# Five pairs of split weights in place of four, the split three granules ahead in place of two, and eight weight buffers in place of nine

## The chip, the cores and the metric

The kernel runs on one core of one Trainium2 chip. The metric is the device time of one execution in microseconds. The engines are TensorE (PE; its weight loads are shown as PEld), VectorE (DVE), ScalarE (ACT), GpSimd (POOL) and SyncE (SP), which issues most DMA transfers.

## The reference

A trunk of two decoder layers on 256 positions of width 1024, in float32. Each layer adds to h, one after the other, a half-step SwiGLU FFN, a token mixer (differential attention in layer 0, a Mamba-2 SSD mixer in layer 1), a cross-attention into 256 memory tokens, and another half-step FFN; each works on an RMSNorm of h, and a final RMSNorm ends it.

```python
def swiglu(h, w_gate, w_up, w_down):
    return (jax.nn.silu(h @ w_gate) * (h @ w_up)) @ w_down
...
    for i in range(DEPTH):
        h = h + 0.5 * swiglu(rmsnorm(h, ffn1_norm[i]), ffn1_w_gate[i], ffn1_w_up[i], ffn1_w_down[i])
        hn = rmsnorm(h, mix_norm[i])
        ...
        h = h + memory_cross_attention(rmsnorm(h, xa_norm[i]), mem, xa_mem_norm[i],
                                       xa_w_q[i], xa_w_kv[i], xa_w_o[i])
        h = h + 0.5 * swiglu(rmsnorm(h, ffn2_norm[i]), ffn2_w_gate[i], ffn2_w_up[i], ffn2_w_down[i])
    return rmsnorm(h, final_norm)
```

An FFN has 2816 hidden units. All weights are read from HBM once, as float32.

## The kernel before

**The split.** Nearly every product with a weight is made of three matmuls on a shorter float format (`mm3`, lines 261 to 264): the weight and the other operand are each split into a high and a low part, and high by high, high by low and low by high are summed in PSUM. A weight arrives as a tile `w` of 128 partitions by 2048 (1 MB) in one of the buffers of pool `wp`. It is used in two *granules* of 1024 columns (class `Gran`; a few are smaller). `Gran.split` takes one pair of buffers from pool `hp`, loads the weight if that is not done yet, casts it on ACT to the high part `whi` (line 224), and subtracts on DVE to get the low part `wlo` (line 225; two granules of the very first product do it on POOL):

```python
            hi = hp.tile([P, 1024], F32R, name="whi", tag="hi")
            lo = hp.tile([P, 1024], F32R, name="wlo", tag="lo")
            ...
                nc.scalar.copy(hv, src)
                self.eng.tensor_tensor(self.lo[:, :, o:o + n], src, hv.bitcast(F32), op=ALU.subtract)
```

A pair is free again when the granule's last matmul is done, and a weight buffer when its last granule's low part is done.

**The lookahead.** The products are listed as `units`; all their granules stand in one list in the order of use, and each knows its place `at`. A product takes its granules through `use`, which first writes down the splits of all granules up to AHEAD further ones:

```python
    def ready(n):
        while done[0] < min(len(grans), n):
            grans[done[0]].split()
            done[0] += 1

    def use(gr):
        for g in gr:
            ready(g.at + AHEAD + 1)
            yield g
```

`last`, the final FFN's tail, calls `ready(gr[-1].at + AHEAD)` itself. Work that follows a product (moving results out of PSUM, transposes, softmax and so on) is put down through `pipe`, a clock of estimated PE time: a piece is written when the PE work written so far has reached its due time.

**Order.** In the first two units (the gate and the up product of the first 512 hidden columns) PE, DVE, ACT and SP run their instructions in the order in which they are written (`manual_schedule`). Afterwards the compiler's scheduler chooses each engine's order from priorities and its own estimates; in the SSD part PE's order is the written one again. At run time every engine works through its own queue.

**The start.** `begin` issues the first loads (the first weight in four pieces of 256 KB with the second half of x between them, then the second weight in two of 512 KB), writes the first four of eight rows of the normalized input (`xh`, `xl`, from `put`) and the splits of granules 0 to 2. The gate unit's eight granules have one row (512 columns) each. The other rows 4 to 7 come from `second`, due at 2.7 us of the pipe's clock, each with the splits up to its row (`ready(k + 1)` for rows 4 and 5); the squares for the norm's scale are due at 2.6 and 7.0.

**The FFN's blocks.** Most of the gate and up products are done in blocks of seven half-size products instead of eight (`seven`, lines 361 to 393). A block loads four weight tiles, of which some products need sums: `x1` is the sum of two tiles (`Sum.load`, line 203, on DVE, into a buffer of its own), `x2` adds a third to it (line 203 again, in place), `x3` and `x4` add by DMA from POOL's queue (line 199). A granule of a block is six matmuls of 512 columns; between them `share` puts granules of plain products with twelve matmuls, which need as much splitting for twice the matmul work. There are three such blocks in the first FFN, four in each of the other three, and one in each cross-attention.

Of the kernel before, what the change touches and what calls it, by code (L numbers as in the profile page):

```python
# [20 lines left out]
NHT = HID // P  # L21
EPS = 1e-6

AHEAD = 2

T = dict(gate=5.5, hid=3.0, turn=1.3, row=5.0, rot=5.5, probs=(1.0, 4.0, 7.0, 10.0), tp=8.5, heads=4.5, otp=6.5,
         xprobs=5.0, xtp=5.5, xo=3.0, evac=1.5)
# [30 lines left out]
def trunk(ctx, tc, a, out):  # L58
# [1 line left out]


    const = ctx.enter_context(tc.tile_pool(name="const", bufs=1))
    wp = ctx.enter_context(tc.tile_pool(name="wp", bufs=9))
    hp = ctx.enter_context(tc.tile_pool(name="hp", bufs=4))
    xp = ctx.enter_context(tc.tile_pool(name="xp", bufs=8))
    sp = ctx.enter_context(tc.tile_pool(name="sp", bufs=28))
    wk = ctx.enter_context(tc.tile_pool(name="wk", bufs=7))
# [163 lines left out]
# [11 lines that stand above are left out]
# [1294 lines left out]
    def last(norm):  # L1536
# [56 lines left out]
        def run(*gr):  # L1593
            ready(gr[-1].at + AHEAD)
            last_ = gr[-1].k0 + gr[-1].nk == 20
            for t, c0, c1 in [(0, 0, 512), (1, 0, 256), (1, 256, 512)]:
                if (t, c0) not in banks:
                    banks[t, c0] = acc("fin")[:, :c1 - c0]
                b = banks[t, c0]
                for g in gr:  # L1600
                    for k in range(g.nk):
                        kt = g.k0 + k
                        mms(b, t, g, k, slice(c0, c1), kt, kt == 12, kt == 19)
                if last_:
                    for q in range((c1 - c0) // 256):
                        evac(b[:, q * 256:(q + 1) * 256], t, 2 + c0 // 256 + q)
# [80 lines left out]
```

## Time and profile before

| | |
|---|---|
| median of 3 runs | 1257.57 us (1257.47 to 1257.57) |
| the profiled execution | 1258.38 us, span of its instructions 1256.6 us |
| busy: PE, PEld, DVE, ACT, POOL | 1247.1, 1071.7, 1057.2, 873.5, 162.5 us |
| granted clock | 0.999 |
| casts to high parts (line 224, ACT) | 534, 551.0 us |
| subtractions to low parts (line 225, DVE) | 532, 639.4 us |
| sums of weights (line 203, DVE) | 32, 73.2 us |
| read from HBM | 271.72 MB, 218 GB/s over the span |

Rows of the timeline give the start in us from the span's start, the length in us, the engine (a q behind its name: its queue issuing a DMA), the line, the operation, what it writes and reads, the shape, and in brackets how long the engine had been idle and what ended that. Rows of waits give who waited for whom, the sum in us, how often, and the longest. Rows of windows give the stretch, its length, each engine's busy time and number of instructions (PE, PEld, DVE, ACT, POOL), the granted clock, the mean busy share of the 16 DMA engines, and GB/s. Rows of groups give count, busy us, mean ns of one, and the engine's idle time just before them with what ended most of it.

### The profile page before, as it was taken

Reading aid. Unit: us, or ns where it says so; the run is one execution under the profiler, and the core shown is the slowest. Engines: PE = TensorE matmul, PEld = TensorE weight load, DVE = VectorE, ACT = ScalarE, POOL = GpSimd, SP = SyncE. Lnnn points to the kernel's source line nnn. Section 1 sums busy time; section 2 is a strip of 40 time slices with the busy share of each in tenths; the row PEclk is TensorE's granted clock in tenths of the full one; section 3 lists DMA queues with packets and bytes.
Section 4 is the critical chain, followed back from the end, with each engine's and each line's share of the span. In section 5 each row is a group of like instructions: output and inputs, shape, how many; then the busy total and the mean of one; then the engine's idle time right before and its main releaser. Section 6 shows DMA issues by size and latency. Waiting matters only on the chain.

```text
span 1256.6 us, 18186 instructions
## 1 busy us (share of the span) xinstructions
PE 1247.1 (99%) x6751; PEld 1071.7 (85%) x6751; DVE 1057.2 (84%) x1451; ACT 873.5 (70%) x1388; POOL 162.5 (13%) x139
## 2 busy tenths in 40 slices
PE   9999999999999999999999999999999999999997
PEld 7888888788998888888888889999998898888886
DVE  6998787887787999887998976798898887898886
ACT  6676764686676776767776756777876775877772
POOL 1101102101101111110111000022233100011100
PEclk9999999999999999999999999999999999999999
DMA  9989976445776688987879977665636586489961
GB/s 330 301 255 259 314 256 208 137 165 170 222 214 170 165 252 260 293 246 234 240 198 268 311 247 221 192 193 168 201 134 185 169 246 182 157 251 256 258 190 34
DMA packets 161195, 275.03 MB, mean 219 GB/s; under 512 B 7209, under 2 KB 43730, under 8 KB 161106
## 3 DMA queue, kind: packets, MB, share of 16 engines
q1 hardware_dynamic: 137744, 229.75, 53.4%
q0 software_dynamic: 19744, 38.28, 17.7%
q10 hardware_dynamic: 3618, 5.84, 1.4%
q8 instruction: 53, 0.87, 0.3%
q14 instruction: 36, 0.29, 0.1%
HBM read 271.72 MB, written 2.13 MB: 218 GB/s over the span
## 4 chain that ended last, share of the span: by engine, by line
PE 94%; DMA 2%; DVE 2%; ACT 2%; issue 1%; POOLq 0%; POOL 0%; SPq 0%; ACTq 0%; DVEq 0%
PE out L262 9%; PE out L264 9%; PE out L263 9%; PE seven L263 8%; PE seven L262 8%; PE seven L264 8%; PE htp L855 1%; PE up L263 1%; PE up L264 1%; PE up L262 1%; PE xs L264 1%; PE xs L262 1%; PE xq L263 1%; PE xq L264 1%; PE xs L263 1%; PE xq L262 1%
## 5 line engine op out<-in xcount | busy, mean ns | idle before, releaser
L225 DVE TENSOR_TENSOR wlo<-w,whi 128x1024 fp32r<-128x1024 f32 (+2 forms) x532 | 639.4, 1220 | 134.6 <-ACT whi L224 126.8
L224 ACT CAST whi<-w 128x1024 fp32r<-128x1024 f32 (+2 forms) x534 | 551.0, 1039 | 245.2 <-PE out L264 84.0
L262 PE MATMUL out<-whi,hid_hi 128*128 128x512 f32 x336 | 132.3, 394 | 0.0
L264 PE MATMUL out<-whi,hid_lo 128*128 128x512 f32 x336 | 131.0, 390 | 0.0
L263 PE MATMUL out<-wlo,hid_hi 128*128 128x512 f32 x336 | 130.8, 389 | 0.0
L263 PE MATMUL seven<-wlo,s_hi 128*128 128x512 f32 x272 | 106.0, 390 | 0.6 <-DVE wlo L225 0.6
L262 PE MATMUL seven<-whi,s_hi 128*128 128x512 f32 x272 | 106.2, 390 | 0.0
L264 PE MATMUL seven<-whi,s_lo 128*128 128x512 f32 x272 | 105.9, 389 | 0.0
L199 POOL DMA_DIRECT2D w<-in_ffn_w_up_dram x30 | 36.7, 1268 | 346.6 <-DVE wlo L225 339.5
L203 DVE TENSOR_TENSOR w<-w 128x2048 f32<-128x2048 f32 x32 | 73.2, 2287 | 2.0 <-DMA w<-in_ffn_w_gate_dram 1.5
L264 PEld LDWEIGHTS out<-whi,hid_lo 128*128 128x128 f32 x336 | 63.1, 188 | 13.4
L263 PEld LDWEIGHTS out<-wlo,hid_hi 128*128 128x128 f32 x336 | 63.1, 188 | 12.6
L262 PEld LDWEIGHTS out<-whi,hid_hi 128*128 128x128 f32 x336 | 63.1, 188 | 12.5
L262 PE MATMUL seven<-whi,xh 128*128 128x512 f32 x180 | 70.5, 392 | 0.0
L264 PE MATMUL seven<-whi,xl 128*128 128x512 f32 x180 | 70.1, 389 | 0.0
L263 PE MATMUL seven<-wlo,xh 128*128 128x512 f32 x180 | 70.0, 389 | 0.0
L263 PEld LDWEIGHTS seven<-wlo,s_hi 128*128 128x128 f32 x272 | 51.1, 188 | 11.4 <-DVE wlo L225 1.0
L264 PEld LDWEIGHTS seven<-whi,s_lo 128*128 128x128 f32 x272 | 51.1, 188 | 10.7
L262 PEld LDWEIGHTS seven<-whi,s_hi 128*128 128x128 f32 x272 | 51.1, 188 | 10.4
L199 POOL DMA_DIRECT2D w<-in_ffn_w_gate_dram x30 | 36.9, 1467 | 176.2 <-DVE xst L1146 62.3
L264 PEld LDWEIGHTS seven<-whi,xl 128*128 128x128 f32 x180 | 33.8, 188 | 7.1
L262 PEld LDWEIGHTS seven<-whi,xh 128*128 128x128 f32 x180 | 33.8, 188 | 6.8
(395 smaller groups left out, 3013.7 us busy)
## 6 DMA issues: line engine op xcount, KB each, us to landing
w<-in_ffn_w_up_dram SPq DMA_DIRECT2D x40, 1024.0 KB, 7.8
w<-in_ffn_w_down_dram SPq DMA_DIRECT2D x40, 1024.0 KB, 9.3
w<-in_ffn_w_gate_dram SPq DMA_DIRECT2D x38, 1024.0 KB, 8.9
w<-in_ssd_w_in_dram SPq DMA_DIRECT2D x24, 1024.0 KB, 5.4
w<-in_xa_w_kv_dram SPq DMA_DIRECT2D x16, 1024.0 KB, 6.4
w<-in_ffn_w_gate_dram POOLq DMA_DIRECT2D x30, 512.0 KB, 9.7
w<-in_ffn_w_up_dram POOLq DMA_DIRECT2D x30, 512.0 KB, 7.2
w<-in_da_w_in_dram SPq DMA_DIRECT2D x12, 1024.0 KB, 5.2
```

The costliest lines, as they stand in the source:

```text
L199: nc.gpsimd.dma_start(self.t[:, k:k + 2, :], w.src[r0:r0 + 2 * P, w.c0:w.c0 + w.n] .rearrange("(k p) c -> p k c", p=P), accum_op=ALU.add)
L203: nc.vector.tensor_tensor(self.t, self.l.t, w.t, op=ALU.add)
L224: nc.scalar.copy(hv, src)
L225: self.eng.tensor_tensor(self.lo[:, :, o:o + n], src, hv.bitcast(F32), op=ALU.subtract)
L262: nc.tensor.matmul(o, lhsT=lh, rhs=rh, start=start, stop=False, skip_group_check=onto)
L263: nc.tensor.matmul(o, lhsT=lh, rhs=rl, start=False, stop=False, skip_group_check=onto)
L264: nc.tensor.matmul(o, lhsT=ll, rhs=rh, start=False, stop=stop, skip_group_check=onto)
L855: nc.tensor.transpose(tp[:, j, t * P:(t + 1) * P], us[t][:, (i + j) * P:(i + j + 1) * P], ident)
```

## The change

One pair of `hp` buffers more (a pair of 1024 and 1024 columns), one `wp` buffer of 2048 columns less, and AHEAD is 3: `use` writes the splits of three granules beyond the one in use.

```diff
-AHEAD = 2
+AHEAD = 3
...
-    wp = ctx.enter_context(tc.tile_pool(name="wp", bufs=9))
-    hp = ctx.enter_context(tc.tile_pool(name="hp", bufs=4))
+    wp = ctx.enter_context(tc.tile_pool(name="wp", bufs=8))
+    hp = ctx.enter_context(tc.tile_pool(name="hp", bufs=5))
```

## The prediction

> **What bounds the kernel now.** I read the page's busy row first, then the windows of the busy times, and then the waits of TensorE (PE).
>
> ```profile
> span 1256.6 us, 18186 instructions
> PE 1247.1 (99%) x6751; PEld 1071.7 (85%) x6751; DVE 1057.2 (84%) x1451; ACT 873.5 (70%) x1388; POOL 162.5 (13%) x139
> 0.00:31.40 31.40, 29.60 (x125) 22.03 (x126) 20.21 (x38) 20.41 (x37) 6.22 (x11) 1.00 0.97 331
> 31.40:62.80 31.40, 30.77 (x142) 25.23 (x141) 28.94 (x35) 19.43 (x26) 5.03 (x4) 1.00 0.99 301
> 502.40:533.80 31.40, 31.40 (x144) 26.12 (x143) 27.96 (x27) 22.90 (x26) 3.44 (x4) 1.00 0.98 294
> 1224.60:1256.00 31.40, 25.22 (x138) 21.72 (x136) 21.06 (x52) 9.86 (x13) 1.13 (x2) 0.95 0.10 34
> ```
>
> PE is idle for 9.5 us of 1256.6: 1.80 in the first window, 0.63 in the second, about 6 in the last; 502.4 to 533.8 shows a stretch in the middle, without any. A busy PE can still hide small waits, because the modelled end of a matmul (0.39 us long) lies behind the next one's start. So the starts have to be compared:
>
> ```profile
> 56.69 0.39 PE L264 MATMUL gate<-whi,xl 128*128 128x512 f32 x1
> 56.92 0.39 PE L262 MATMUL seven<-whi,s_hi 128*128 128x512 f32 x1
> 57.93 0.50 PE L263 MATMUL seven<-wlo,s_hi 128*128 128x512 f32 x1 [0.63 <-DVE wlo L225]
> 58.27 0.40 PE L264 MATMUL seven<-whi,s_lo 128*128 128x512 f32 x1
> 19.48 0.39 PE L262 MATMUL up<-whi,xh 128*128 128x512 f32 x1
> 19.98 0.50 PE L263 MATMUL up<-wlo,xh 128*128 128x512 f32 x1
> 20.32 0.40 PE L264 MATMUL up<-whi,xl 128*128 128x512 f32 x1
> ```
>
> A 512-column matmul starts 0.23 us after the one before (56.69 to 56.92). Here are the two places where PE waits for a low part: 0.78 + 0.11 us too much at 57, 0.27 + 0.11 at 20. I found no later matmul of a streamed weight that waits so long for its split. That is all the split's lookahead can win: about 1.3 us.
>
> ```profile
> ACT whi L224 <- PE out L264: 84.0, 64, 1.7
> ACT whi L224 <- PE seven L264: 46.7, 123, 2.2
> SPq L161 <- DVE wlo L225: 790.4, 158, 15.8
> L203 DVE TENSOR_TENSOR w<-w 128x2048 f32<-128x2048 f32 x32 | 73.2, 2287 | 2.0 <-DMA w<-in_ffn_w_gate_dram 1.5
> ```
>
> The chain of waits says the same from the other side. ACT's casts stand idle (84.0 + 46.7 us) until PE frees a pair: the four pairs are full, the split is paced by PE. SP waits 790 us for low parts to be finished, because only that frees a weight buffer: the loads are paced by buffers, and the change takes one away.
>
> The Trainium skill (Perfetto Trace Analysis, Identifying Performance Opportunities) says that a gap repeating on the engine that should be saturated can mean too few buffers for the next tile. Here such gaps are on ACT, and PE has none in 502 to 534; by that rule, as by the rows, a fifth pair alone wins nothing in the middle of the kernel.
>
> **The change part by part.** No instruction is added or removed on PE; casts, subtractions and loads keep their number. What moves is their order.
>
> *A. The first unit.* ACT, DVE, SP and PE keep the written order there. Now `use` for granule 1 calls ready(5) in place of ready(4), so the cast of granule 4 goes ahead of the two squares and of xh for rows 4 and 5:
>
> ```profile
> 9.43 0.62 ACT L224 CAST whi<-w 128x512 fp32r<-128x512 f32 x1 [0.74 <-DMA w<-in_ffn_w_gate_dram]
> 10.32 0.61 ACT L224 CAST whi<-w 128x512 fp32r<-128x512 f32 x1
> 10.83 0.63 ACT L513 ACTIVATE sq<-h 128x512 f32<-128x512 f32 x1
> 12.07 0.46 ACT L457 ACTIVATE xh<-xt,cols 128x256 fp32r<-128x256 f32 x1
> 12.43 0.61 ACT L224 CAST whi<-w 128x512 fp32r<-128x512 f32 x1
> 13.45 0.61 ACT L224 CAST whi<-w 128x512 fp32r<-128x512 f32 x1
> 11.01 1.29 POOL L225 TENSOR_TENSOR wlo<-w,whi 128x512 fp32r<-128x512 f32 x1 [7.00 <-ACT whi L224]
> 14.14 1.29 POOL L225 TENSOR_TENSOR wlo<-w,whi 128x512 fp32r<-128x512 f32 x1 [1.84 <-ACT whi L224]
> 13.99 0.39 PE L262 MATMUL gate<-whi,xh 128*128 128x512 f32 x1
> 15.58 0.40 PE L263 MATMUL gate<-wlo,xh 128*128 128x512 f32 x1
> 9.00:12.00 3.00, 3.00 (x19) 2.58 (x18) 1.63 (x4) 2.57 (x7) 0.99 (x1) 1.00 1.05 408
> 17.63 3.88 ACT L224 CAST whi<-w 128x1024 fp32r<-128x1024 f32 x4
> ```
>
> Granule 4's cast runs at 12.43 now; moved, it stands behind that of 10.32 and can start at 10.83 if its weights are there. They are the 512 KB behind the first weight's four 256 KB pieces. The third piece ended ACT's wait at 9.43; 768 KB follow it in the queue, at the window's 408 GB/s 1.93 us, so they land near 11.4 (my estimate). ACT, strictly in order, then waits 0.57 us with the squares and xh queued behind, and everything behind comes 0.57 + 0.51 (one cast's pitch, 10.32 to 10.83) = 1.08 us later. Row 4 bears that (its xh then ends at 12.07 + 0.46 + 1.08 = 13.61, and PE takes it at 13.99). Row 5 does not: its cast at 13.45 and its low part on POOL end at 14.14 + 1.29 = 15.43, 0.15 before the matmul that reads it (15.58). So PE waits 1.08 - 0.15 = **+0.93**. Bounds: weights there by 10.83, shift 0.51, wait 0.36; weights there only at 12.43, shift 2.11, wait 1.96. I take 0.93, the transfer being priced by its own window. The squares feed the gate's scale much later and cost nothing.
>
> *B. The up unit.* PE arrives 0.93 later and the first of the four casts at 17.63 now stands ahead of the second pair of squares, so its low part is ready: the 0.27 + 0.11 go, **-0.38** (bounds -0.38 and 0).
>
> *C. The first block of seven products, at 57.* PE missed a low part by 0.78 us. It comes 0.55 later (A and B), and ACT starts each cast one granule earlier, which DVE can follow as far as it had idle time:
>
> ```profile
> 24.00:46.00 22.00, 22.00 (x103) 18.27 (x102) 20.36 (x35) 13.05 (x18) 0.00 (x0) 1.00 1.05 384
> 53.20 2.28 DVE L203 TENSOR_TENSOR w<-w 128x2048 f32<-128x2048 f32 x1
> 56.66 5.77 DVE L225 TENSOR_TENSOR wlo<-w,whi 128x1024 fp32r<-128x1024 f32 x5 [1.17 <-ACT whi L224]
> ```
>
> That is 22.00 - 20.36 = 1.64 us; 0.55 + 1.64 is over 0.89, though the sum at 53.20 stays in front of the subtraction. I take **-0.80** (bounds -0.89 and 0).
>
> *D. Everything after 63 us.* Splits run one granule further ahead; PE, already fed, gains nothing: **0**. The cover is PE's own continuous work; were it gone, the price would be that of the next part.
>
> *E. Eight weight buffers.* Each load waits for one more buffer to come free. At the start that hides: the ninth buffer is filled at 22.11, long after the first could be freed (11.01 + 1.29 = 12.30, the fourth granule's low part on POOL). Later it matters most where the left and right halves of a weight are added on DVE (L203), since that addition needs a load that arrived just before:
>
> ```profile
> 22.11 1.41 SPq L161 DMA_DIRECT2D w<-in_ffn_w_gate_dram  x1
> 460.76 0.37 SPq L161 DMA_DIRECT2D w<-in_ffn_w_gate_dram  x1
> 467.81 2.29 DVE L203 TENSOR_TENSOR w<-w 128x2048 f32<-128x2048 f32 x1
> 470.62 3.48 DVE L225 TENSOR_TENSOR wlo<-w,whi 128x1024 fp32r<-128x1024 f32 x3
> 471.91 0.37 SPq L161 DMA_DIRECT2D w<-in_ffn_w_down_dram  x1
> 472.42 0.39 PE L262 MATMUL out<-whi,hid_hi 128*128 128x512 f32 x1
> 488.94 1.05 ACT L224 CAST whi<-w 128x1024 fp32r<-128x1024 f32 x1 [1.66 <-PE out L264]
> ```
>
> The load of 460.76 feeds the sum of 467.81, in a buffer freed at that moment. With one buffer fewer it goes when the next comes free; the sum's own tile took that one, at 467.81: 7.05 us later. The sum needs a buffer too, the next at 471.91. It would run near 475 and end near 477. Its first split is the cast of 488.94, which moves ahead by at most one granule of twelve matmuls (12 x 0.23 = 2.8): 9 us remain. So **0**, if the sum moves along in DVE's queue. After the first two units DVE's order is the compiler's, which places an operation where it expects its inputs; 32 sums idled DVE for 2.0 us in all, which speaks for its expectation. The additions on POOL's queue start behind splits and sums that shift alike. Bounds of E: 0, and the price of rival 1.
>
> Sum: 0.93 - 0.38 - 0.80 = -0.25 us. The profiled execution took 1258.38 (span 1256.6 and 1.8 around it); 1258.38 - 0.25 = 1258.1. It stands 0.81 above the median of the three runs, so against that median **1257.3 us**.
>
> **The rivals.** *1. Slower: DVE's queue blocks.* If the sum stays where it is in DVE's order, DVE waits for the later load, up to 7.05 us, and the subtractions behind wait too. The first of the three at 470.62 ends near 470.62 + 3.48 / 3 = 471.8 and PE reads its granule at 472.42: 0.6 in hand, plus 2.8 by the further granule. PE then stands 7.05 - 0.6 - 2.8 = 3.7 us, and one place is more than a measurement tells. The later three FFNs have twelve such sums, four in each; all of them give 44 us, 1301 us. It decides as soon as a load comes over 3.4 us behind its sum's place. For it: DVE is 89% busy at 502 to 534, with DMA at 0.98. Against it: the 2.0 us, and the 9 us of room.
>
> The Trainium skill (TensorE: Matmul & The Clock Gate, Architectural detail) states that ACT and DVE are strict FIFO. The trace agrees in part A's rows, where the squares stand behind a cast that waits; by that rule a late sum blocks all behind it, which is this rival's mechanism.
>
> *2. Faster: the start loses nothing.* If part A's weights are there by 10.83, A is 0.36, B and C go in full: 0.36 - 0.38 - 0.89 = -0.9, 1256.7. Even all of PE's idle time of the first two windows is 1.80 + 0.63 = 2.43 us, 1255.1; more would have to come from the last window, whose final matmuls, scaling and output transfers the change doesn't touch. So this stays within no change too, except by a reordering that I can't see.
>
> *3. The change does not do what it says.* ACT's casts stay behind PE, one granule further on; A to C come out at nothing: 1257.6.
>
> **How the numbers follow.** 0.2% is 2.5 us, about what a measurement of this kernel can tell from no change. My forecast with rivals 2 and 3 (all between 1255.1 and 1259.5, the upper end being A's 1.96 with B and C at 0) has 0.84: forecast 0.60, rival 2 0.12, rival 3 0.12. Rival 1 has 0.11, and an unseen gain beyond 2.43 us 0.05. The range is 1255.1 to 1260.3, the upper end with one block 0.8 us short beside A's worst.
>
> **What would show it.** Right: ACT's waits for PE still near 130 us, the gap at 57 gone, the low part of row 5 late by about 1 us near 15.6, SP's wait for buffers longer, L203 still idle under 5 us, PE without gaps after 63. Wrong: PE waiting for wlo inside a block of seven after 63 us behind a sum that waited for a load (rival 1), or PE's busy time itself shorter than 1247 by more than 2.

## The result: 1277.15 us, 1.5% slower

| | before | changed |
|---|---|---|
| median, same chip | 1257.57 us | 1277.15 us (1276.3 to 1277.37) |
| ratio, 95% interval | | 1.0153 [1.014, 1.0165] |
| profiled execution, span | 1258.38, 1256.6 us | 1276.3, 1274.5 us |
| busy PE | 1247.1 us | 1253.2 us |

The forecast was 1257.3 (1255.1 to 1260.3): no change. It came out as rival 1, slower by a blocked DVE queue, though not with the victim that the rival named. The median stands 0.85 us above the profiled execution; all traces below are of profiled executions.

**Where the time went.** The transposes that open each stage's normalization (L535) are the same rows in both kernels, so their starts show how far behind the changed kernel is. First the kernel before, then the changed one, from each timeline of PE:

```profile
405.27 1.04 PE L535 MATMUL xt<-ident,h 128*128 128x128 f32 x8
571.73 1.03 PE L535 MATMUL xt<-ident,h 128*128 128x128 f32 x8
759.79 1.04 PE L535 MATMUL xt<-ident,hn 128*128 128x128 f32 x8
990.20 1.03 PE L535 MATMUL xt<-ident,h 128*128 128x128 f32 x8
1076.09 1.04 PE L535 MATMUL xt<-ident,h 128*128 128x128 f32 x8
```

```profile
405.59 1.04 PE L535 MATMUL xt<-ident,h 128*128 128x128 f32 x8
576.18 1.04 PE L535 MATMUL xt<-ident,h 128*128 128x128 f32 x8
768.67 1.04 PE L535 MATMUL xt<-ident,hn 128*128 128x128 f32 x8
1002.88 1.03 PE L535 MATMUL xt<-ident,h 128*128 128x128 f32 x8
1088.74 1.04 PE L535 MATMUL xt<-ident,h 128*128 128x128 f32 x8
```

Behind by 0.32, 4.45, 8.88, 12.68 and 12.65 us, and by 17.9 at the end of the span. So the first 400 us, all of the start included, cost 0.32; the second feed-forward step (405 to 572) 4.13, the third 4.43, the SSD part (760 to 990) 3.80, the cross-attention behind it nothing, and the fourth feed-forward step with the tail 5.25. Most of each is one place, a stop of PE at 441, 620, 942 and 1125 us; the second step has a smaller one besides, of the same kind (a sum at 477.51 waits 1.80 us for its load, the subtraction L831 stands behind it in DVE's queue, ACT's copy L832 waits for that, and PE waits 0.69 us at 482.21). The list of what PE waited for in the changed kernel names the four stops, and the groups and ACT's and SP's waits answer to the rows shown of before:

```profile
PE htp L855 <- DVE gs L808: 8.4, 6, 2.9
PE pcb L1412 <- DVE c L1363: 2.3, 1, 2.3
ACT whi L224 <- PE out L264: 88.1, 71, 2.0
ACT whi L224 <- PE seven L264: 38.0, 105, 1.9
SPq L161 <- DVE wlo L225: 841.4, 164, 17.2
L203 DVE TENSOR_TENSOR w<-w 128x2048 f32<-128x2048 f32 x32 | 73.2, 2287 | 21.2 <-DMA w<-in_ffn_w_gate_dram 20.7
```

The last row is the signature: the sums of weights idled DVE for 20.7 us on the gate weights' loads, against 1.5 before.

**One of the three stops.** Rows of the changed kernel's timeline around 438 us (SP's queue, DVE, PE):

```profile
429.03 0.37 SPq L161 DMA_DIRECT2D w<-in_ffn_w_gate_dram  x1
430.92 2.59 DVE L225 TENSOR_TENSOR wlo<-w,whi 128x1024 fp32r<-128x1024 f32 x2 [0.78 <-ACT whi L224]
437.97 2.29 DVE L203 TENSOR_TENSOR w<-w 128x2048 f32<-128x2048 f32 x1 [4.47 <-DMA w<-in_ffn_w_gate_dram]
440.18 1.40 DVE L808 SCALAR_TENSOR_TENSOR gs<-up,rcol,gs 128x512 f32<-128x512 f32 x2
438.24 0.39 PE L264 MATMUL gateup<-whi,xl 128*128 128x512 f32 x1
440.98 0.33 PE L855 MATMUL htp<-ident,gs 128*128 128x128 f32 x1 [2.35 <-DVE gs L808]
441.64 0.98 PE L855 MATMUL htp<-ident,gs 128*128 128x128 f32 x7 [0.33 <-DVE gs L808]
```

The load goes out at 429.03, when a weight buffer comes free, and the sum starts at 437.97. DVE stands idle from 433.5, because its queue holds the sum in front of L808, the multiply of gate and up. The data of L808 are complete near 435.2 (PE's last matmul of `up` starts at 434.84 and takes 0.39), but it starts at 440.18. PE reaches the transposes of that product (htp) and stands. The same place in the kernel before:

```profile
419.48 15.64 SPq L161 DMA_DIRECT2D w<-in_ffn_w_gate_dram  x2
430.17 2.29 DVE L203 TENSOR_TENSOR w<-w 128x2048 f32<-128x2048 f32 x1
434.65 1.40 DVE L808 SCALAR_TENSOR_TENSOR gs<-up,rcol,gs 128x512 f32<-128x512 f32 x2
```

There the sum stands ahead of L808 too, but its load went out at 419.48 (the row takes two loads together, the second is at 434.76) and it never waits. The load is 9.55 us later in the changed kernel. The sum has moved behind the two subtractions that stood between, and now stands directly ahead of L808.

**What a stop costs besides itself.** The stop of the fourth feed-forward step, on PE:

```profile
1121.39 0.39 PE L264 MATMUL gateup<-whi,xl 128*128 128x512 f32 x1
1124.64 0.33 PE L855 MATMUL htp<-ident,gs 128*128 128x128 f32 x1 [2.86 <-DVE gs L808]
1126.04 0.75 PE L262 MATMUL gateup<-whi,xh 128*128 128x512 f32 x1
1126.58 0.63 PE L263 MATMUL gateup<-wlo,xh 128*128 128x512 f32 x1
1127.01 0.63 PE L264 MATMUL gateup<-whi,xl 128*128 128x512 f32 x1
1129.77 0.39 PE L262 MATMUL seven<-whi,s_hi 128*128 128x512 f32 x1
```

From 1121.39 to 1124.64 pass 3.25 us in place of 0.23. Then matmuls start 0.43 us apart (1126.58 to 1127.01), nearly twice the usual pitch: the nine from 1126.04 to 1129.77 take 3.73 us where 9 x 0.23 = 2.07 would do. Stop 3.02 and slow matmuls 1.66 make 4.68 of the stage's 5.25; most of the rest is the second wait of htp, behind the first of its transposes. The granted clock shows the slow matmuls (windows of the changed kernel; the last three numbers are clock, DMA share, GB/s):

```profile
596.60:628.00 31.40, 28.89 (x125) 23.67 (x124) 24.78 (x23) 19.47 (x24) 4.93 (x4) 0.95 0.62 144
1099.00:1130.40 31.40, 28.21 (x121) 22.91 (x120) 23.46 (x24) 19.55 (x24) 4.90 (x4) 0.95 0.60 145
```

### The profile page after: what moved, and what is told of

Its sections match the earlier page's. It is cut to its first block, busy times and chain, and to the rows that moved or that the text cites. A ratio compares the mean times of both kernels' runs of the same rounds, so it can differ in the third digit from the quotient of the medians.

```text
span 1274.5 us, 18212 instructions
## 1 busy us (share of the span) xinstructions
PE 1253.2 (98%) x6751; PEld 1075.0 (84%) x6751; DVE 1056.6 (83%) x1451; ACT 871.0 (68%) x1388; POOL 161.1 (13%) x139
## 4 chain that ended last, share of the span: by engine, by line
PE 81%; DVE 7%; ACT 4%; DMA 3%; issue 3%; POOL 1%; SPq 0%; POOLq 0%; DVEq 0%; ACTq 0%
PE out L264 9%; PE out L262 9%; PE out L263 9%; PE seven L263 7%; PE seven L262 7%; PE seven L264 7%; DVE wlo L225 3%; DMA w<-in_ffn_w_gate_dram 3%; ACT whi L224 2%; PE htp L855 2%; PE mk L262 1%; PE mk L264 1%; PE xq L264 1%; PE xq L263 1%; PE mk L263 1%
## 5 line engine op out<-in xcount | busy, mean ns | idle before, releaser
L224 ACT CAST whi<-w 128x1024 fp32r<-128x1024 f32 (+2 forms) x534 | 549.1, 1039 | 245.3 <-PE out L264 88.1
L203 DVE TENSOR_TENSOR w<-w 128x2048 f32<-128x2048 f32 x32 | 73.2, 2287 | 21.2 <-DMA w<-in_ffn_w_gate_dram 20.7
L263 PEld LDWEIGHTS seven<-wlo,s_hi 128*128 128x128 f32 x272 | 51.1, 188 | 11.4 <-DVE wlo L225 1.1
L858 ACT CAST hid_hi<-htp 128x512 fp32r<-128x512 f32 x44 | 24.6, 590 | 31.3 <-PE htp L855 31.0
```

What stands on the lines that cost most here:

```text
L203: nc.vector.tensor_tensor(self.t, self.l.t, w.t, op=ALU.add)
L263: nc.tensor.matmul(o, lhsT=lh, rhs=rl, start=False, stop=False, skip_group_check=onto)
L858: nc.scalar.copy(hi, tp)
```

## The experiments

Theory Q: eight buffers make loads late, and that is the loss. Theory L: the lookahead of three puts sums and splits where they block. Theory I, later J: two parts must meet, an early place in DVE's queue and a late load; I has the early place from the lookahead, J from the fifth pair. Theory K: five pairs cost by themselves. Each median is set against the kernel before on the same chip (1257.8 to 1258.0).

**1. Eight buffers alone** (against before: `wp` bufs 9 to 8).

> Eight weight buffers alone; four pairs and the split two granules ahead stay as before. Theory Q (too few weight buffers: loads are issued 7 to 9 us later, and DVE stands at a sum, L203, whose load has not landed, with the multiply L808 behind it): most of the loss is here too, 1268 to 1275 us, with DVE idle 15 us or more ahead of L203 on the gate weights' load (20.7 us in the changed kernel, 1.5 before). Theory L (the split three ahead puts sums and splits into DVE's queue ahead of what PE waits for): 1257.6 within 1 us, L203 idle under 5 us. Theory I (only both together: a later load and an earlier place of the sum): 1257 to 1261, L203 idle 2 to 8 us.

1261.05 us, ratio 1.0026 [1.0017, 1.0036].

```profile
115.58 2.29 DVE L203 TENSOR_TENSOR w<-w 128x2048 f32<-128x2048 f32 x1 [4.13 <-DMA w<-in_ffn_w_gate_dram]
119.07 0.50 PE L263 MATMUL seven<-wlo,xh 128*128 128x512 f32 x1 [1.95 <-DVE wlo L225]
438.74 1.41 DVE L808 SCALAR_TENSOR_TENSOR gs<-up,rcol,gs 128x512 f32<-128x512 f32 x2
444.67 2.28 DVE L203 TENSOR_TENSOR w<-w 128x2048 f32<-128x2048 f32 x1
```

Q and L are out in their simple form; I comes nearest (its upper end, and 7.0 us of idle DVE ahead of L203). Where the changed kernel stops, the sum here comes behind L808 (444.67 after 438.74): it did move along, as step E assumed. The trace shows one other place, in the first feed-forward step: a sum 4.13 us late, and behind it the low part of a block of seven. The profiled execution, at 1262.67 us the slowest of ten, loses 3.8 us by 185 us of its span, slow matmuls behind the stop included; the median loses 3.2. That is rival 1's chain, in the one feed-forward step that the rival had not counted.

**2. Five pairs and eight buffers, two ahead** (the changed kernel with `AHEAD = 2`).

> Five pairs and eight weight buffers, split two granules ahead. Against the changed kernel only the lookahead is undone. Q: as with eight buffers alone, 1268 to 1275 us. L: 1257.6 within 1 us, and the stop of TensorE at 939 us on c (2.42 us) is gone. I: 1257 to 1261. In all three the first unit's wait for the fifth row's low part (0.8 us) is gone, since granule 4 is cast in its old place.

1273.09 us, 1.012 [1.0105, 1.0135]. The number is Q's, but not for Q's reason: the fifth pair, which I had priced at nothing, adds 12.0 us to the 3.2 of the eight buffers. The stops are those of the changed kernel: PE waits 8.1 us in 6 for gs, and the sum is back in front of L808. The lookahead isn't needed for them, so I's 1257 to 1261 is out as well: the sum's early place comes with the fifth pair, and from here on the theory is J. With two ahead the wait of the first unit and the stop at 939 us are gone, as expected; the changed kernel has them besides.

**3. Three ahead, four pairs, nine buffers** (against before: `AHEAD = 3`).

> Split three granules ahead with four pairs and nine weight buffers. Q: the three stops of 2.5 to 3 us at the first product block of the later feed-forward steps (438, 618, 1121 us) are gone, what stays is the first unit's 1.1 us and the stop at 939 us with its slow matmuls, 3 to 6 us: 1260 to 1264. L: nearly the whole loss, 1272 to 1277. I: as Q, or less: 1258 to 1264; L203 idle under 5 us.

1259.58 us, 1.0015 [1.0006, 1.0024]; L203 idles DVE 1.4 us. L is out. The 1.7 us lie mostly at the start (step A).

**4. and 5. Nine buffers with five pairs**, two and three ahead. A ninth weight buffer, 8 KB of each partition, had to be paid for by four of the 28 row tiles of pool `sp` (2 KB each); with three of them there is no room, since pool `sm` needs 5.81 KB of a partition where 4.84 would be left. The edit is against the changed kernel; the first of the two also has `AHEAD = 2`.

```diff
-    wp = ...bufs=8
-    sp = ...bufs=28
+    wp = ...bufs=9
+    sp = ...bufs=24
```

> Five pairs and nine weight buffers, split two ahead as before, sp with 24 tiles. J: 1257 to 1260 us, L203 idle under 5 us. K: 1268 to 1274, as with eight buffers (1273.1).

> Five pairs, split three ahead, and nine weight buffers; for their room the small row pool, sp, has 24 tiles in place of 28, which is a change of its own. Known by now: eight buffers alone cost 3.2 us, five pairs with eight 15.2, three ahead with nine and four pairs 1.7. Theory J (only five pairs and eight buffers together stop DVE: five pairs let the sum stand early in its queue, eight buffers bring its load late): the three stops of 2.4 us ahead of the transposes (438, 618, 1121 us) are gone, 1258 to 1262 us, DVE idle under 5 us ahead of L203. Theory K (five pairs cost by themselves, by the order they give): 1268 to 1277.

1269.06 us, 1.0094 [1.0078, 1.0109], and 1269.94 us, 1.0098 [1.0081, 1.0115]. Three ahead adds 0.9, which the spread of the runs (1268.43 to 1271.48 with two ahead) doesn't tell from nothing. J's 1257 to 1260 and 1258 to 1262 are missed, and by the times alone K would have it. The trace of the first (two ahead) says otherwise:

```profile
431.39 2.28 DVE L203 TENSOR_TENSOR w<-w 128x2048 f32<-128x2048 f32 x1
437.00 1.40 DVE L808 SCALAR_TENSOR_TENSOR gs<-up,rcol,gs 128x512 f32<-128x512 f32 x2
PE pcb L1412 <- DVE c L1363: 6.7, 1, 6.7
```

The sum is early as with eight buffers, its load is there, and none of the three stops is left. Most of the loss is one stop at another place, in the SSD part, with slow matmuls behind it. A smaller part is J's own chain at a fourth place: in the first feed-forward step a sum waits 3.71 us for its load (it starts at 111.79), and PE waits 1.75 us at 115.87 for the low part behind it. For the stop in the SSD part a control was needed.

**6. The control: before with 24 tiles in `sp`**, nothing else.

> The kernel before with 24 tiles in the small row pool in place of 28, nothing else: the control for the two runs with nine buffers and five pairs, which lose 11.2 and 12.1 us and nearly all of it at one stop of 6.7 us ahead of pcb at 939 us. If the 24 tiles make that stop: 1266 to 1270 us, with the same stop. If the five pairs make it: 1257 to 1260.

1266.32 us, 1.0066 [1.0051, 1.0081], with the same stop (ACT, then PE):

```profile
927.57 0.91 ACT L1486 ACTIVATE y<-y,yrc 128x256 f32<-128x256 f32 x2 [3.47 <-POOL yrc L466]
936.67 1.23 PE L1412 MATMUL pcb<-c,b 128*128 128x128 f32 x4 [6.50 <-DVE c L1363]
```

The 24 tiles make it: ACT's queue holds a scaling that waits for POOL in front of the casts and of the work on c. Against this control five pairs cost 1269.06 - 1266.32 = 2.7 us with nine buffers, against 1273.09 - 1261.05 = 12.0 with eight. Of the 2.7 us, 2.2 are there by 182 us of the span, behind that late sum. J stands, with the control in place of the uncorrected numbers: five pairs cost little where the loads come in time. The comparison is between kernels with 28 row tiles on the one side and 24 on the other; with 28, nine buffers and five pairs don't fit.

**7. The victim moved out of the way.** In the changed kernel the transposes of the product are written later on the order's clock (`pipe`'s clock of estimated PE time), so that PE does other matmuls first:

```diff
-                pipe.after(T["hid"], lambda: turn(c, us, n))
+                pipe.after(T["hid"] if o or norm is first_norm else 6.5, lambda: turn(c, us, n))
```

> The changed kernel with one number altered: in the three later feed-forward steps the transposes of the first hidden block (L855) are put 6.5 us of the order's clock behind the up product in place of 3.0, so that TensorE has its next matmuls ahead of them. DVE's queue and the loads stay. J's chain (load late, sum L203 waits, multiply L808 behind it, transposes behind that): the waits of TensorE for gs (8.4 us in 6) go, and with each the slow clock behind it: three places at 2.7 to 5 us, 1262 to 1269 us, while DVE's idle time ahead of L203 stays near 20 us. If the low parts behind the same sum are what TensorE really needs, the stop only moves to a wait for wlo: 1272 to 1277.

1273.64 us, 1.0129 [1.0112, 1.0146]: only 3.5 us come back.

```profile
442.84 0.50 PE L263 MATMUL seven<-wlo,s_hi 128*128 128x512 f32 x1 [1.59 <-DVE wlo L225]
```

No wait for gs is left, and PE waits for the next low part behind the same sum instead: the second of the two expectations. What is blocked is a queue; taking one victim out shows the next.

**8. All sums held in their written place.**

```diff
-                nc.vector.tensor_tensor(self.t, self.l.t, w.t, op=ALU.add)
+                tc.keep_in_program_order(nc.vector.tensor_tensor(self.t, self.l.t, w.t, op=ALU.add))
```

> The changed kernel with every sum L203 held behind the DVE instruction that the program writes just before it, so that it can't be queued ahead of its turn; loads, buffers and lookahead stay. If the early place of the sum in DVE's queue is what makes a late load stop everything: the stops at 438, 618 and 1121 us go, DVE idle ahead of L203 falls from 20.7 us to under 6, and 1262 to 1267 us stay (the stop at 939 us and the first unit's remain). If the late load itself is what TensorE waits for (eight buffers): ACT's casts and TensorE's low parts wait in its place, 1272 to 1277. The new order may open a stop elsewhere, which the idle stretches of TensorE would show.

1268.3 us, 1.0082 [1.0067, 1.0097], 8.9 us less than the changed kernel with the same eight buffers.

```profile
L203 DVE TENSOR_TENSOR w<-w 128x2048 f32<-128x2048 f32 x32 | 73.0, 2282 | 0.0
```

No sum waits for a load any more and the three stops are gone. New small ones open (PE waits 3.7 us in 7 for low parts of a block of seven, 1 of them there before), which is why 1268.3 lies just above the forecast of 1262 to 1267.

**9. The same hold in the kernel before.**

> The kernel before with every sum L203 held behind the DVE instruction written just before it. The sums of the kernel before stood early without being late (DVE idle 1.5 us ahead of them), so no wait goes: 1257.6 within 1 us; if a sum in its written place comes too late for its own cast, TensorE waits for low parts of seven: 1259 to 1264.

1291.33 us, 1.0261 [1.0244, 1.0278], far beyond both expectations.

```profile
PE seven L263 <- DVE wlo L225: 11.6, 16, 0.8
PE seven L262 <- ACT whi L224: 5.9, 6, 1.1
```

With four pairs and two ahead a sum in its written place is too late for its own cast, at 16 places and more; ACT's casts wait 40.6 us for DVE's sums, against 11.7 in the kernel before. The early place that the compiler gives a sum is worth 33 us there. With held sums the change as a whole (1268.3 against 1291.33) gains 23. That fits the view that the lookahead it buys was there already, made by the reordering; it isn't shown beyond these two times.

**10. Only the three sums held, and the first two units split two ahead.** `x1` of the second block (`c == 2`) in the later three feed-forward steps is held as in 8; `use` takes 2 in place of AHEAD until the first two units are written.

> The changed kernel with two of the causes taken out where they act: only the three sums that stopped DVE at 438, 618 and 1121 us (the first sum of the second product block in the later feed-forward steps) are held behind the DVE instruction written before them, and the first two units are split two ahead as before, the rest three ahead. If the causes add up: the three stops with the slow clock behind them (8 to 10 us) and the first unit's 1.1 us go, 1265.5 to 1268.5 us; the stop at 939 us stays unless the new order moves it. Had holding all 32 sums gained something besides, less goes here: 1269 to 1273. A version better than the kernel before (under 1257 us) is expected by neither.

1266.71 us, 1.0076 [1.0059, 1.0092], as expected from the sum of the causes. Its timeline (lines are five further on here):

```profile
404.55 1.04 PE L540 MATMUL xt<-ident,h 128*128 128x128 f32 x8
572.31 1.03 PE L540 MATMUL xt<-ident,h 128*128 128x128 f32 x8
451.00 2.29 DVE L204 TENSOR_TENSOR w<-w 128x2048 f32<-128x2048 f32 x1
```

The second feed-forward step takes 167.76 us, against 170.59 in the changed kernel and 166.46 before. The held sum runs at 451.00, 13 us later than where it blocked, and PE hardly misses it: one new wait of 0.39 us, at 463.83, for a low part behind the next sum of the same block, and one as long at each of the other two places. PE didn't need the late load at the time of the stop, only the queue did. DVE still idles 14.9 us ahead of other sums, most of them with nothing urgent behind; the longest (3.94 us, the sum at 1182.28) has PE waiting 1.43 us for a low part.

**11. A sum made by DMA.** In the changed kernel `second` is "dma" for the first block in the later feed-forward steps.

> The changed kernel with the second sum of the first product block of the three later feed-forward steps (the L203 that stands at 438, 618 and 1121 us) made by two accumulating DMAs from POOL's queue (L199), the way the other sums go, so that it is no longer in DVE's queue. J: the multiply L808 runs in its place, the three stops go, DVE idle ahead of L203 falls from 20.7 to some 7 us; 1262 to 1269 us. If the accumulating DMAs land later than the sum was made, ACT's cast and TensorE wait for them instead, 3 to 6 us at each place: 1276 to 1285.

1285.29 us, 1.0219 [1.0204, 1.0235]. The edit moved the wrong sum, as experiment 10 later showed: it took `x2` of the first block, and the sum that blocks is `x1` of the second.

```profile
440.52 2.29 DVE L203 TENSOR_TENSOR w<-w 128x2048 f32<-128x2048 f32 x1 [4.19 <-issue]
```

The blocking sum is still there, 2.55 us later than in the changed kernel, and PE waits 14.6 us for gs in place of 8.4. It says nothing on the forecast it was made for, but a loss that grows with the sum's delay is in keeping with J.

**12. The product of c and b (two inputs of the SSD part) later in PE's order**, 16 in place of 12 on the order's clock.

> The changed kernel with one place in the order altered: the product of c and b (L1412, pcb) that waits 2.3 us for c at 939 us is put 4 us of the order's clock later. If that stop and the slow clock behind it are as large as read from the trace (2.7 us of stop, about 2 to 3 us of slow matmuls): 1270.5 to 1273 us, and the window from 910 to 973 us has no idle TensorE. If the slow clock has another cause than the stop ahead of it: the stop goes and the clock of 0.95 in 942 to 973 us stays, 1274 to 1275.

1276.04 us, 1.0138 [1.0123, 1.0154]: at best some 1 us better, within the spread of its four runs (1272.55 to 1277.41), and not 4 to 7. Both expectations are missed. The wait on c went, and the transposes of xs (a third input) a little further on wait 1.6 us for DVE in its place. As in 7, the victim moved and the queue stayed. What the slow clock there comes from isn't tested by it, since a stop remained.

No version beats the kernel before. Experiment 10 is the best with five pairs and eight buffers and is still 0.8% slower.

## Why the prediction was wrong, step by step

**A** held. The cast of granule 4 did wait for its weights (0.52 us, until 11.03, in an execution whose ACT rows stand 0.42 us earlier; I had estimated 0.57, until 11.4), and the fifth row's low part came late: from row to row PE lost 1.10 us at 14.9 (forecast 0.93). **B** held: at 20 us the three matmuls of `up` start 0.23 us apart and the gap is gone. **C** failed at a small price. The rows at 57 us in the changed kernel:

```profile
57.24 0.39 PE L262 MATMUL seven<-whi,s_hi 128*128 128x512 f32 x1
58.26 0.50 PE L263 MATMUL seven<-wlo,s_hi 128*128 128x512 f32 x1 [0.63 <-DVE wlo L225]
```

That is 1.02 - 0.23 = 0.79 us, as before. The sum that feeds this granule stands at 53.52, 0.32 later than before like everything around it: the split further ahead did not bring the sum forward. I had named that sum as standing in front, and then took the gain all the same. What held it at its place isn't settled. The start together came to +0.32 against -0.25, and even that is part luck: PE reached row 5 0.50 us earlier in this execution than in that of the kernel before (14.85 against 15.35). Executions differ by about as much without the change: the control of experiment 6, whose start is split two ahead as before, passes the first row of the list above at 404.83, 0.44 us before the kernel before. Without that head start A to C come to about +0.8.

**D** was right from 63 to 400 us and for the cross-attentions, and wrong in the SSD part, where I looked at casts and low parts of weights alone and not at what else stands in their queues. There the changed kernel has three low parts in front of c (DVE 941.01), one of which waits for its cast, and PE stops for 2.26 us, with slow matmuls behind: 3.80 us. What c needs from ACT is ready at 940.37, so the last of the three low parts explains 0.6 us of the stop; the rest of the delay isn't taken apart. The stop is absent with five pairs and eight buffers two ahead (experiment 2), 1.7 us in experiments 7 and 10, and 6.5 us in the control, which changed four row tiles alone. So it follows the order that the compiler arrives at; which part of the change tips it isn't settled beyond that.

**E** is the step that failed. "0, if the sum moves along in DVE's queue": with eight buffers alone it does (experiment 1), with five pairs too it doesn't get behind L808 (2). Why the compiler moves it far enough with four pairs and not with five isn't settled. I had priced pairs and buffers one by one, each at nothing; the loss is in their meeting. Room there was (I had worked out 9 us at the sum of 467.81; the sum that blocks runs 13 us later in experiment 10, and PE waits 0.39 us), and it was worthless, because the sum's room doesn't help what stands behind it. And the argument that 32 sums idled DVE for 2.0 us in all, which I took for the compiler's expectation, showed only that loads had come in time with nine buffers.

**Rival 1** had the right mechanism and point of decision (a load more than 3.4 us behind the sum's place; here 4.3 to 5.0) and 0.11. It looked at the subtractions behind the sum, and the first thing to be missed was the multiply L808, with less time in hand; the three stages hit lost 4.1 to 5.3 us each, in place of 3.7, with slow matmuls behind two of the three stops and the wait at 482 us in the other stage. How late a sum is doesn't decide alone: of the others, one late by 1.80 us (at 477.51) cost PE 0.69, and one late by 3.06 (at 114.88, in the first feed-forward step) cost nothing. The rival's mechanism in the Trainium skill (TensorE: Matmul & The Clock Gate, Architectural detail: ACT and DVE strictly first in, first out) agrees with experiments 7 (the victim moved: 3.5 us back) and 8 (the sum held: 8.9).

Of the signs, ACT's waits for PE (88.1 + 38.0, forecast near 130), the late fifth row and SP's longer wait (841.4 against 790.4) came as said; L203's idle time (20.7, forecast under 5) and PE's gaps after 63 us gave the forecast away, and the gap at 57 stayed. The first three fit both outcomes; only L203's idle time and the later gaps could tell them apart. Rival 1's own sign, PE waiting for wlo inside a block of seven after 63 us, didn't come in the changed kernel; it came in experiments 1 and 7.

## What to carry to other kernels

Where a compiler orders a queue, look for the operations it places early, and ask of each not how much room it has itself but what stands behind it and how soon that is needed; a change that delays its input by more than that turns the room into a stop. Buffer counts are not independent knobs: one pair more cost 12.0 us beside eight weight buffers and 2.7 beside nine (these with 24 row tiles), and four spare row tiles less cost 8.4 with nothing else changed, so a size traded for another needs a control of its own. When a wait is found, fix the place of the operation that blocks the queue, not the operation that is seen waiting.

## What the hardware showed besides

A stop of PE of about 2 us or more was often followed by 1 to 4 us of matmuls at nearly half speed: after 1.95 us (experiment 1, windows' clock 0.95), 2.18 and 2.86 us (the changed kernel at 620 and 1125) and 6.50 us (the control). But it didn't follow from the length alone. In the changed kernel the clock stayed at 1.00 after the 2.35 us at 441 (window 439.60 to 471.00), and in experiment 12:

```profile
1121.52 0.33 PE L855 MATMUL htp<-ident,gs 128*128 128x128 f32 x1 [2.89 <-DVE gs L808]
1099.00:1130.40 31.40, 28.18 (x128) 22.84 (x126) 25.45 (x24) 20.62 (x26) 4.90 (x4) 1.00 0.61 131
```

After 2.89 us the clock stayed at 1.00. The Trainium skill (TensorE: Matmul & The Clock Gate, What's actually happening) has the clock halved after an idle window of about 3.4 us, the windows running freely; by that rule 1.95 us would be safe, and the measurement decides against it. Free windows would fit that equal stops end differently, but no run here shows the windows themselves. It may also be why kernels with such stops spread wider (experiment 12: 1272.55 to 1277.41) than the kernel before (1257.65 to 1258.76); that was not tested.
